# A hybrid S5 and retention decoder layer: first-stage loads one k-tile at a time, fused sine and cosine polynomials, squares moved to ScalarE, earlier side work

## The chip, the cores and the metric

The kernel runs on one core of one Trainium2 chip. The metric is the device time of one execution in microseconds (us); the median of the runs is compared. The engines are TensorE (PE for its matmuls, PEld for its weight loads), VectorE (DVE), ScalarE (ACT), GpSimd (POOL) and SyncE (SP), which here only issues DMAs. Each engine executes its own instructions in the order of the program and waits on semaphores for the others.

## The reference

One decoder layer on 256 prompt positions and on 8 sequences of 8 new positions each, 320 columns in all, at a model width of 2048:

```
h = rms_norm(x, norm_mix)
u, q, k, v, g = split(h @ w_in)
lam_bar = exp(lam * exp(log_step))                 # complex, 64 groups x 64 states
b_bar   = ((lam_bar - 1) / lam) * b
s5      = scan over positions of x' = lam_bar * x + b_bar u;  y = Re(c x) + d * u; gelu; sigmoid GLU
ret     = chunked retention, 8 heads, rotary q and k, group norm, silu(g) gate
x = x + concat(s5, ret) @ w_out
x = x + (silu(gate) * up) @ w_ffn_out              # gate, up = rms_norm(x) @ w_ffn_in
return rms_norm(x), the S5 end states, the retention end states
```

## The kernel before, in words

**Matmuls.** Activations lie transposed: 128 features by 320 columns. Each fp32 weight block `raw` is split into a rounded part `hi` (a copy by ACT) and the rest `lo = raw - hi` (by DVE), the activations likewise into `xhi` and `xlo`; a product is three matmuls: hi with xhi, hi with xlo, lo with xhi. `wload` (L124) and `gemm` (L139) do this for eight k-tiles at a time. The rings `raw`, `hi` and `lo` have three buffers each.

**First stage** (L929 to L957). Four column blocks of `w_in` are accumulated at once over 16 k-tiles of 128 input features: 12 matmuls per k-tile, into `py`, the two halves of `pb`, and `ps_p`. Per step SP loads `x` into `xrs` (the tiles `u32` and `retp`) and then the weights into `raw`; ACT makes `xhi` (L272), `hi` (L943) and the squares for the norm (L277); DVE makes `xlo` (L273), `lo` (L944) and adds the squares up in `u32` (L279 to L288). The steps are the k-tiles 0, 1, then pairs. SP's order in this loop is the order of the code, so a weight load that waits for its `raw` buffer holds the loads behind it. After the loop, PE runs two k-tiles of the next product, `ps_pv`, then six small matmuls `ps_r` that sum the squares (L205), then the rest of `ps_pv`.

**S5 parameters beside it.** `s5_exps` (L374) runs 47 POOL instructions on 128x32 values: 23 for `dt_ = exp(log_step)`, one product, 23 for `rr = exp(lam_re * dt_)`. `s5_params` (L383) makes angles from `dt_` and their sines and cosines with polynomials on DVE; `s5_params2` and `s5_params3` (L423, L435) make the powers `lp`, `gp`, `ff` and the fourth power `r4` of `rr`. `first_states` (L472) multiplies the start states by a power on POOL into `lx0`; it is a generator that runs when a clock of the program, `clk`, reaches `T0 + 12`.

**What sets the order.** PE and POOL run in the order of the code. ACT, DVE, and SP outside the first loop, are ordered when the program is built, by priorities (`tc.high_priority(offset=...)`) and an estimate of when inputs are ready. `tc.issue_after(i)` keeps instructions behind `i` on the engine of `i`. The built order is fixed; on the chip an engine whose next instruction waits holds all that stands behind it.

**Later places of the change.** `do_k` (L876) copies the new columns of k to `ksp` on POOL, which `head_k` (L718) multiplies on PE. `s5_chunk` (L579) runs for eight chunks c; SP shifts a Toeplitz tile `toe` with six small DMAs (L649), loads `yc` from DRAM with eight (L683), and PE multiplies `toe` (L660). The tail (L1356 to L1414) normalises and stores three row tiles; `scale` (L1348) is shared out between DVE and POOL, and `keep_warm(12)` (L1397) fills PE while the last root is computed.

Of the kernel before, what the change touches and what calls it, by code (L numbers as in the profile page):

```python
# [46 lines left out]
def hybrid_kernel(ctx, tc, xT, w_in, w_in4, w_out, w_glu, w_fi, w_fo, w_fot, gfr, vecs, s5p, bc, x0,  # L47
# [335 lines left out]
    def s5_params(dt_):  # L383
# [21 lines left out]
        tt(q, q, ang, MUL)
        tt(es[:, 0::3], q, par, MUL)
        q = T(she)
        ts(q, a2, -1.0 / factorial(14), MUL, 1.0 / factorial(12), ADD)
        for kk in (10, 8, 6, 4, 2, 0):
            tt(q, q, a2, MUL)  # L410
            ts(q, q, (1.0 if (kk // 2) % 2 == 0 else -1.0) / factorial(kk), ADD)
        tt(ec[:, 0::3], q, par, MUL)
        for l in range(2):
# [9 lines left out]
    def s5_params2(used):  # L423
        newscr(1)
        scr[1] = used
        tt(lp[:, 0, 0], rr, ec[:, 0], MUL)
        tt(lp[:, 1, 0], rr, es[:, 0], MUL)
        den = tt(T(sh), prm[:, 0], prm[:, 0], MUL)
        d2 = tt(T(sh), prm[:, 1], prm[:, 1], MUL)
        tt(den, den, d2, ADD)  # L430
        rden = T(sh)
        dve.reciprocal(rden, den)
        rot_t["rden"] = rden

    def s5_params3():  # L435
        rden = rot_t["rden"]
        nr = ts(T(sh), lp[:, 0, 0], -1.0, ADD)
        t1 = tt(T(sh), nr, prm[:, 0], MUL)
# [19 lines left out]

        def ri(t, i):
            return (t[:, 0, i], t[:, 1, i])  # L460

        def rep_(t, n):
            return tuple(t[:, q].unsqueeze(1).to_broadcast([P, n, NPAIR]) for q in range(2))

        cmul(ri(lp, 1), ri(lp, 0), ri(lp, 0), sh)
        cmul(ri(lp, slice(2, 4)), rep_(lp[:, :, 1], 2), ri(lp, slice(0, 2)), [P, 2, NPAIR])
        cmul(ri(gp, slice(0, 3)), rep_(ff, 3), ri(lp, slice(0, 3)), [P, 3, NPAIR])

# [110 lines left out]
    def s5_chunk(c):  # L579
# [64 lines left out]
        with tc.high_priority(offset=EVAC):  # L644
            act.copy(toe[:, :, CH - 1], pk_[:, 0:64].rearrange("p (q h) -> p q h", h=16))
        for u in range(2):
            for t in range(CH - 1):
                d = 16 * (CH - 1 - t)
                sp.dma_start(toe[64 * u + d:64 * u + 64, :, t], toe[64 * u:64 * u + 64 - d, :, CH - 1])  # L649
        with tc.high_priority(offset=2 * EVAC if c == 7 else 0):  # L650
# [28 lines left out]
        yc = s5.tile([P, CH, NC], F32, name="yc", tag="yc", bufs=1)  # L679
        for j in range(4):  # L680
            for g in range(2):
                r = 32 * j + 16 * g
                sp.dma_start(yc[r:r + 16], back[j % 2, :, :, j // 2, g].rearrange("t h c -> h t c"))  # L683
        yield DL["y"]
# [59 lines left out]
    def head_v(h, v_, qg, rt, R):  # L744
# [611 lines left out]
    with tail_order:  # L1356
# [39 lines left out]
        store(1, 0, 5)  # L1396
# [120 lines left out]
```

## Time and profile before

| | |
|---|---|
| runs shown, us | 1429.81, 1428.19, 1428.51: median 1428.51 |
| the profiled execution's own time, us | 1427.82 |
| its span, first to last instruction, us | 1426.0 (1.82 lie around it) |
| granted TensorE clock, mean | 0.999 |
| DVE, ACT, POOL busy | 958.0, 606.4, 124.6 us |
| DMA queue q1 | 264.91 MB, 55.9% of 16 engines |

How to read it: the share of busy time is an average over the stages of the kernel. What a change in one stage can bring is read from the waits of the engine that sets the end in that stage, and from the timeline around them. Times in the timeline are us from the start of the span, then the duration; in brackets is the idle time before the instruction and what ended it. In a table of groups stand busy time and mean ns of one, then the idle time before them. In a table of windows stand, for each engine, busy us and the number of instructions, then the granted clock as a share.

### The profile page before, as it was taken

To read this page: it belongs to the slowest core of one execution; us is meant where nothing else is said; L and a number is where in the kernel's file an instruction comes from. 1 tells how busy PE (TensorE), PEld (TensorE's weight loads), DVE (VectorE), ACT (ScalarE), POOL (GpSimd) and SP (SyncE) were. 2 spreads that over 40 slices of the span, in tenths; PEclk is the share of its full clock that TensorE was granted. 3 is DMA by queue.
4 is the path that set the end of the run, shared out by engine and by line. 5 is a ranking of instruction groups with operands and counts; after the bars stand their busy time and mean duration, and the time that the engine had idled before them with its cause. 6 is when DMAs were issued, how large, how long until landed. Compare 5 with 4: busy or idle time off the path is not lost.

```text
span 1426.0 us, 26198 instructions
## 1 busy us (share of the span) xinstructions
PE 1416.9 (99%) x10376; PEld 1406.4 (99%) x10376; DVE 958.0 (67%) x1852; ACT 606.4 (43%) x965; POOL 124.6 (9%) x194
## 2 busy tenths in 40 slices
PE   9999999999999999999999999999999999999998
PEld 8999999999999999999999999999999999999998
DVE  7978888787657756777777545767744677645453
ACT  7645555555445443333333333333333333333452
POOL 7530021110000000000001000000000000000002
PEclk9999999999999999999999999999999999999999
DMA  8555555556544466675656446666545765455442
GB/s 289 172 170 167 159 174 154 172 163 205 169 154 149 164 207 229 222 254 199 245 201 236 136 147 240 233 213 240 167 144 183 252 230 188 154 165 179 150 142 74
DMA packets 102315, 267.07 MB, mean 187 GB/s; under 512 B 27376, under 2 KB 42160, under 8 KB 102192
## 3 DMA queue, kind: packets, MB, share of 16 engines
q1 hardware_dynamic: 101824, 264.91, 55.9%
q8 instruction: 81, 1.33, 0.4%
q10 hardware_dynamic: 368, 0.49, 0.1%
q14 instruction: 42, 0.34, 0.1%
HBM read 254.44 MB, written 10.52 MB: 186 GB/s over the span
## 4 chain that ended last, share of the span: by engine, by line
PE 76%; DVE 1%; issue 0%; ACT 0%; DMA 0%; SPq 0%; DVEq 0%; ACTq 0%
PE ps_fu L146 7%; PE ps_fg L146 7%; PE ps_fg L145 7%; PE ps_fu L145 7%; PE ps_fg L147 7%; PE ps_fu L147 7%; PE ps_fo L146 7%; PE ps_fo L145 7%; PE ps_fo L147 7%; PE ps_o L145 2%; PE ps_o L147 2%; PE ps_o L146 2%; PE ps_t L1315 1%; PE ps_g L147 1%; PE ps_g L145 1%; PE ps_g L146 1%
## 5 line engine op out<-in xcount | busy, mean ns | idle before, releaser
L133 ACT CAST hi<-raw 128x1024 fp32r<-128x1024 f32 (+1 forms) x410 | 397.8, 971 | 680.9 <-PE ps_fg L146 184.8
L135 DVE TENSOR_TENSOR lo<-raw,hi 128x1024 fp32r<-128x1024 f32 (+1 forms) x410 | 462.2, 1128 | 303.9 <-ACT hi L133 301.8
L147 PE MATMUL ps_fg<-hhi,lo 128*128 128x320 f32 x704 | 217.5, 309 | 0.0
L145 PE MATMUL ps_fg<-hhi,hi 128*128 128x320 f32 x704 | 217.5, 309 | 0.0
L146 PE MATMUL ps_fg<-hlo,hi 128*128 128x320 f32 x704 | 217.5, 309 | 0.0
L146 PE MATMUL ps_fu<-hlo,hi 128*128 128x320 f32 x704 | 217.5, 309 | 0.0
L145 PE MATMUL ps_fu<-hhi,hi 128*128 128x320 f32 x704 | 217.5, 309 | 0.0
L147 PE MATMUL ps_fu<-hhi,lo 128*128 128x320 f32 x704 | 217.5, 309 | 0.0
L145 PE MATMUL ps_fo<-ahl,hi 128*128 128x320 f32 x671 | 207.6, 309 | 0.0
L146 PE MATMUL ps_fo<-ahl,hi 128*128 128x320 f32 x671 | 207.3, 309 | 0.0
L147 PE MATMUL ps_fo<-ahl,lo 128*128 128x320 f32 x671 | 207.3, 309 | 0.0
L145 PE MATMUL ps_p<-xhi,hi 128*128 128x320 f32 x560 | 177.3, 317 | 0.0
L147 PE MATMUL ps_p<-xhi,lo 128*128 128x320 f32 x560 | 173.0, 309 | 0.0
L146 PE MATMUL ps_p<-xlo,hi 128*128 128x320 f32 x560 | 172.8, 309 | 0.0
L147 PEld LDWEIGHTS ps_fg<-hhi,lo 128*128 128x128 f32 x704 | 132.1, 188 | 0.0
L146 PEld LDWEIGHTS ps_fg<-hlo,hi 128*128 128x128 f32 x704 | 132.1, 188 | 0.0
L145 PEld LDWEIGHTS ps_fu<-hhi,hi 128*128 128x128 f32 x704 | 132.1, 188 | 0.0
L146 PEld LDWEIGHTS ps_fu<-hlo,hi 128*128 128x128 f32 x704 | 132.1, 188 | 0.0
L147 PEld LDWEIGHTS ps_fu<-hhi,lo 128*128 128x128 f32 x704 | 132.1, 188 | 0.0
L145 PEld LDWEIGHTS ps_fg<-hhi,hi 128*128 128x128 f32 x704 | 132.1, 188 | 0.0
L146 PEld LDWEIGHTS ps_fo<-ahl,hi 128*128 128x128 f32 x671 | 126.0, 188 | 0.0
L145 PEld LDWEIGHTS ps_fo<-ahl,hi 128*128 128x128 f32 x671 | 125.9, 188 | 0.0
(497 smaller groups left out, 2118.2 us busy)
## 6 DMA issues: line engine op xcount, KB each, us to landing
raw<-w_fi SPq DMA_DIRECT2D x176, 512.0 KB, 4.2
raw<-w_in SPq DMA_DIRECT2D x79, 512.0 KB, 4.1
raw<-w_fo SPq DMA_DIRECT2D x61, 512.0 KB, 3.4
raw<-w_out SPq DMA_DIRECT2D x32, 512.0 KB, 3.7
hi<-vd SPq DMA_DIRECT2D x32, 512.0 KB, 5.5
lo<-vd SPq DMA_DIRECT2D x32, 512.0 KB, 5.2
raw<-w_fo SPq DMA_DIRECT2D x61, 192.0 KB, 2.4
rt<-r SPq DMA_DIRECT2D x8, 512.0 KB, 5.6
```

Of the source, the lines that this page charges most:

```text
L133: cast = act.copy(hi[:, :m], raw[:, :m])
L135: last_lo[0] = dve.tensor_tensor(lo[:, :m], raw[:, :m], f(hi[:, :m]), SUB)
L145: pe.matmul(ps, hi, xhi[:, k], start=k == 0, stop=False)
L146: pe.matmul(ps, hi, xlo[:, k], start=False, stop=False)
L147: pe.matmul(ps, lo, xhi[:, k], start=False, stop=k == nk - 1)
L1315: pe.matmul(ps[0:m, 0:TC], a3[:, x_, k, s:s + m], w_[:, k], start=k == 0 and x_ == 0 and w_ is whi, stop=k == FCT - 1 and w_ is wlo)
```

## The change

Six edits in one:

1. The first stage's steps are k-tiles 0, 1, 2, 3 singly, then pairs (numbers from 0). From k-tile 4 on, SP issues the weight load ahead of the x load.
2. The polynomials of sine and cosine use one DVE instruction a term (add, then multiply) in place of two; the products in `s5_params3` are done with fewer and larger instructions.
3. Four squares go from DVE to ACT: two of `prm`, and `rr` twice to `r4`. They are written in `s5_params2`, so ahead of `s5_params3`.
4. `first_states` is called at head 0's group norm and has no time of its own any more.
5. The `toe` DMAs of the last chunk and the `yc` DMAs of chunk 6 get priority.
6. In the tail `scale` is shared 4, 5 and 4 blocks in place of 5, 5 and 3, and `keep_warm` is 10.

`s5_params` was and is held behind `los[4]`; in the list of `lo` instructions that was k-tiles 6 and 7, and with two more entries it is k-tiles 4 and 5.

```diff
-        q = T(she)
-        ts(q, a2, 1.0 / factorial(13), MUL, -1.0 / factorial(11), ADD)
-        for kk in (9, 7, 5, 3, 1):
-            tt(q, q, a2, MUL)
-            ts(q, q, (1.0 if (kk // 2) % 2 == 0 else -1.0) / factorial(kk), ADD)
...
+        tt(ang, ang, par, MUL)
+        for dst, top, last in ((es, 13, ang), (ec, 14, par)):
+            q = ts(T(she), a2, (-1.0) ** (top // 2) / factorial(top), MUL)
+            for kk in range(top - 2, 1, -2):
+                stt(q, q, (-1.0) ** (kk // 2) / factorial(kk), a2, ADD, MUL)
+            stt(dst[:, 0::3], q, 1.0, last, ADD, MUL)
...
-        den = tt(T(sh), prm[:, 0], prm[:, 0], MUL)
-        d2 = tt(T(sh), prm[:, 1], prm[:, 1], MUL)
+        den, d2 = T(sh), T(sh)
+        act.activation(den, prm[:, 0], AF.Square)
+        act.activation(d2, prm[:, 1], AF.Square)
+        act.activation(r4, rr, AF.Square)
+        act.activation(r4, r4, AF.Square)
...
-        r2 = tt(T(sh), rr, rr, MUL)
-        tt(r4, r2, r2, MUL)
...
         def first_states():
-
-            yield max(0.0, T0 + 12.0 - clk.now)
             newscr(0)
...
-        spawn(first_states())
+        rot_t["first"] = first_states
...
+        with tc.high_priority(offset=3 * EVAC if c == 7 else 0):
+            for u in range(2):
+                for t in range(CH - 1):
+                    d = 16 * (CH - 1 - t)
+                    sp.dma_start(toe[64 * u + d:64 * u + 64, :, t], toe[64 * u:64 * u + 64 - d, :, CH - 1])
...
+        with tc.high_priority(offset=3 * EVAC if c == 6 else 0):
+            for j in range(4):
...
         pool.tensor_tensor(w_, m_, y_, MUL)
+        if h == 0:
+            rot_t["first"]()
...
-    for k1 in (1, *range(2, KT + 1, 2)):
+    for k1 in (1, 2, 3, *range(4, KT + 1, 2)):
...
-            sp.dma_start(xrs[k0 // 4][:, k0 % 4:(k1 - 1) % 4 + 1], xT[:, k0:k1])
+            def load_x():
+                sp.dma_start(xrs[k0 // 4][:, k0 % 4:(k1 - 1) % 4 + 1], xT[:, k0:k1])
+
+            if k0 < 4:
+                load_x()
             (sp if k0 else act).dma_start(raw[:, q], w_in4[:, k0:k1])
+            if k0 >= 4:
+                load_x()
...
-        scale(dve, 1, 0, 5, pb1)
-        scale(pool, 1, 5, 10, rbt[1])
+        scale(dve, 1, 0, 4, pb1)
+        scale(pool, 1, 4, 9, rbt[1])
...
-        keep_warm(12)
+        keep_warm(10)
...
-        scale(dve, 1, 10, NF, pb1)
+        scale(dve, 1, 9, NF, pb1)
```

**ACT in the first stage.** Before, ACT's rows from the `xhi` of k-tiles 8 and 9 on (`retp` holds the x of k-tiles 8 to 15; `hi<-raw` of 1024 values is a pair's weights; `retp<-retp` is a square for the norm):

```order
L272 ACTIVATE xhi<-retp,vec 128x320 [waits DMAHW4_49]
L272 ACTIVATE xhi<-retp,vec 128x320
L943 CAST hi<-raw 128x1024 [waits DMAHW5_49,PE_49]
L277 ACTIVATE retp<-retp 128x640 [waits DVE_49]
L272 ACTIVATE xhi<-retp,vec 128x320 [waits DMAHW6_49]
L272 ACTIVATE xhi<-retp,vec 128x320
```

The same place after the change (L948 is the cast, L424 and L425 the squares that make `r4`, printed as `r_126`):

```order
L272 ACTIVATE xhi<-retp,vec 128x320 [waits DMAHW7_49]
L272 ACTIVATE xhi<-retp,vec 128x320
L424 ACTIVATE r_126<-rr 128x32 [waits Pool_49]
L948 CAST hi<-raw 128x1024 [waits DMAHW0_49,PE_49]
L277 ACTIVATE retp<-retp 128x640 [waits DVE_49]
L272 ACTIVATE xhi<-retp,vec 128x320 [waits DMAHW1_49]
L272 ACTIVATE xhi<-retp,vec 128x320
L425 ACTIVATE r_126<-r_126 128x32 [waits Activation_49]
```

From k-tile 4 on a pair's cast now stands ahead of its `xhi`, where before it stood behind: the first cast of the first piece is that of k-tiles 8 and 9, the first of the second piece that of k-tiles 10 and 11. Ahead of the latter now stands a square that reads `rr`, POOL's last result of `s5_exps`.

**DVE in the first stage.** Before, DVE's rows from the `xlo` of k-tiles 6 and 7 on:

```order
L273 SCALAR_TENSOR_TENSOR xlo<-u_119,vec,xhi 128x320 [waits DMAHW2_49,Activation_49]
L273 SCALAR_TENSOR_TENSOR xlo<-u_119,vec,xhi 128x320 [waits Activation_49]
L944 TENSOR_TENSOR lo<-raw,hi 128x1024 [waits DVE_49,DMAHW3_49,PE_49,Activation_49]
L273 SCALAR_TENSOR_TENSOR xlo<-retp,vec,xhi 128x320 [waits DMAHW4_49,Activation_49]
L273 SCALAR_TENSOR_TENSOR xlo<-retp,vec,xhi 128x320 [waits Activation_49]
```

After the change (`scrt<-prm,scrt` is the first angle, `lam_im * dt_`; before, it stood behind the `lo` of the loop's last pair):

```order
L273 SCALAR_TENSOR_TENSOR xlo<-u_119,vec,xhi 128x320 [waits DMAHW5_49,Activation_49]
L273 SCALAR_TENSOR_TENSOR xlo<-u_119,vec,xhi 128x320 [waits Activation_49]
L180 TENSOR_TENSOR scrt<-prm,scrt 128x32 [waits DMAHW1_49,Pool_49]
L174 TENSOR_SCALAR scrt<-scrt 128x32 [waits DVE_49]
L174 TENSOR_SCALAR scrt<-scrt 128x32
L176 TENSOR_SCALAR scrt<-scrt 128x96 [waits DVE_49]
L949 TENSOR_TENSOR lo<-raw,hi 128x1024 [waits DMAHW6_49,PE_49,Activation_49]
L273 SCALAR_TENSOR_TENSOR xlo<-retp,vec,xhi 128x320 [waits DMAHW7_49,Activation_49]
```

Four small instructions, the first of which waits for POOL's `dt_`, now stand ahead of the `lo` of k-tiles 8 and 9.

**POOL at the change from head 0 to head 1.** Before (`gy` is head 0's group norm, `qsp` and `ksp` are head 1's copies, the rows on `scrt` and `lx_133` are `first_states`):

```order
L794 TENSOR_TENSOR gy<-mv,gy 128x2
L867 COPY qsp<-q__1059 128x64
L452 TENSOR_TENSOR scrt<-x0t,lp 128x256
L453 TENSOR_TENSOR scrt<-x0t,lp 128x256
L454 TENSOR_TENSOR lx_133<-scrt 128x256
L455 TENSOR_TENSOR scrt<-x0t,lp 128x256
L456 TENSOR_TENSOR scrt<-x0t,lp 128x256
L457 TENSOR_TENSOR lx_133<-scrt 128x256
L880 TENSOR_TENSOR kvf<-k__1142,kdt 128x64
L882 COPY ksp<-k__1142 128x64
```

After the change:

```order
L791 TENSOR_TENSOR gy<-mv,gy 128x2
L445 TENSOR_TENSOR scrt<-x0t,lp 128x256
L446 TENSOR_TENSOR scrt<-x0t,lp 128x256
L447 TENSOR_TENSOR lx_133<-scrt 128x256
L448 TENSOR_TENSOR scrt<-x0t,lp 128x256
L449 TENSOR_TENSOR scrt<-x0t,lp 128x256
L450 TENSOR_TENSOR lx_133<-scrt 128x256
L866 COPY qsp<-q__1054 128x64
L879 TENSOR_TENSOR kvf<-k__1131,kdt 128x64
L881 COPY ksp<-k__1131 128x64
```

The six instructions of `first_states` moved ahead of head 1's `qsp`. PE's order is the same as before but for two matmuls of `keep_warm`.

More of the change, by code (lines that the diff above doesn't have):

```diff
@@ L399, in s5_params @@
         a2 = tt(T(she), ang, ang, MUL)
-        q = T(she)
-        ts(q, a2, 1.0 / factorial(13), MUL, -1.0 / factorial(11), ADD)
-        for kk in (9, 7, 5, 3, 1):
-            tt(q, q, a2, MUL)
-            ts(q, q, (1.0 if (kk // 2) % 2 == 0 else -1.0) / factorial(kk), ADD)
[L405 to L412, printed above, removed]
+        tt(ang, ang, par, MUL)
[4 more added lines that the diff above has]
+            stt(dst[:, 0::3], q, 1.0, last, ADD, MUL)
         for l in range(2):
@@ L436, in s5_params3 @@
         rden = rot_t["rden"]
-        nr = ts(T(sh), lp[:, 0, 0], -1.0, ADD)
-        t1 = tt(T(sh), nr, prm[:, 0], MUL)
+        t1 = stt(T(sh), lp[:, 0, 0], -1.0, prm[:, 0], ADD, MUL)
         t2 = tt(T(sh), lp[:, 1, 0], prm[:, 1], MUL)
@@ L442, in s5_params3 @@
         t3 = tt(T(sh), lp[:, 1, 0], prm[:, 0], MUL)
-        t4 = tt(T(sh), nr, prm[:, 1], MUL)
+        t4 = stt(T(sh), lp[:, 0, 0], -1.0, prm[:, 1], ADD, MUL)
         tt(t3, t3, t4, SUB)
         tt(ff[:, 1], t3, rden, MUL)
-        r2 = tt(T(sh), rr, rr, MUL)
-        tt(r4, r2, r2, MUL)
         def cmul(o, a, b, shape, tt=tt):
@@ L457, in cmul, with cpow @@
             tt(o[1], u1, u2, ADD)
[L459 to L467, printed above, removed]
+        def cpow(o, a, b, n):
+            used = scr[1]
+            shn = [P, 2, n, NPAIR]
+            u1, u2 = (T([P, 2 * n, NPAIR]).rearrange("p (r n) j -> p r n j", r=2) for _ in range(2))
+            for u, q in ((u1, 0), (u2, 1)):
+                tt(u, a, b[:, q].unsqueeze(1).unsqueeze(1).to_broadcast(shn), MUL)
+            tt(o[:, 0], u1[:, 0], u2[:, 1], SUB)
+            tt(o[:, 1], u1[:, 1], u2[:, 0], ADD)
+            scr[1] = used
+        cpow(lp[:, :, 1:2], lp[:, :, 0:1], lp[:, :, 0], 1)
+        cpow(lp[:, :, 2:4], lp[:, :, 0:2], lp[:, :, 1], 2)
+        cpow(gp, lp[:, :, 0:3], ff, 3)
         def b8(a):
@@ L645, in s5_chunk @@
             act.copy(toe[:, :, CH - 1], pk_[:, 0:64].rearrange("p (q h) -> p q h", h=16))
[L646 to L649, printed above, removed]
+        with tc.high_priority(offset=3 * EVAC if c == 7 else 0):
[3 more added lines that the diff above has]
+                    sp.dma_start(toe[64 * u + d:64 * u + 64, :, t], toe[64 * u:64 * u + 64 - d, :, CH - 1])
         with tc.high_priority(offset=2 * EVAC if c == 7 else 0):
@@ L679, in s5_chunk @@
         yc = s5.tile([P, CH, NC], F32, name="yc", tag="yc", bufs=1)
[L680 to L683, printed above, removed]
+        with tc.high_priority(offset=3 * EVAC if c == 6 else 0):
+            for j in range(4):
+                for g in range(2):
+                    r = 32 * j + 16 * g
+                    sp.dma_start(yc[r:r + 16], back[j % 2, :, :, j // 2, g].rearrange("t h c -> h t c"))
         yield DL["y"]
@@ L1392, in hybrid_kernel @@
         act.copy(rbt[1], pb1[:, 0:P])
-        scale(dve, 1, 0, 5, pb1)
-        scale(pool, 1, 5, 10, rbt[1])
+        scale(dve, 1, 0, 4, pb1)
+        scale(pool, 1, 4, 9, rbt[1])
         tok_out(1, tp_o[1], sp)
-        store(1, 0, 5)
-        keep_warm(12)
+        store(1, 0, 4)
+        keep_warm(10)
         x_, g_ = xo[0][0:ms_], xg[0][0:ms_]
@@ L1400, in hybrid_kernel @@
         act.activation(sqj[0:ms_], x_, AF.Square, accum_out=rs[0:ms_, 2:3])
-        scale(dve, 1, 10, NF, pb1)
-        store(1, 5, 10)
-        store(1, 10, NF)
+        scale(dve, 1, 9, NF, pb1)
+        store(1, 4, 9)
+        store(1, 9, NF)
         pool.tensor_tensor(g_, x_, grow[0:ms_], MUL)
```

## The prediction

> **What bounds the kernel now.** First the page's busy times and then the list of what PE waited for:
>
> ```profile
> PE 1416.9 (99%) x10376; PEld 1406.4 (99%) x10376; DVE 958.0 (67%) x1852; ACT 606.4 (43%) x965; POOL 124.6 (9%) x194
> ```
>
> ```profile
> PE warm_ps L118 <- POOL ones L64: 1.1, 1, 1.1
> PE pss L104 <- POOL ksp L882: 0.9, 1, 0.9
> PE py L953 <- ACT hi L943: 0.6, 1, 0.6
> PE py L104 <- DMA toe<-toe: 0.5, 1, 0.5
> PE py L953 <- DVE xhi L180: 0.3, 1, 0.3
> ```
>
> PE is busy 99% of the span, and these five waits, 3.4 us, are all that it waits for. PE's work stays the same but for two matmuls of `keep_warm`, so the change can take away 3.4 us at most. What it can add has no such limit: any engine that holds up PE costs its whole delay. So what is to be read is whether a new wait reaches PE. The order shows two candidates, both in the first stage, both on POOL's `s5_exps`: an ACT square of `rr` ahead of the cast of k-tiles 10 and 11, and a DVE product with `dt_` ahead of `lo` of k-tiles 8 and 9. Timeline of PE and then of POOL in that stage:
>
> ```profile
> 24.12 0.31 PE L953 MATMUL py<-xhi,hi 128*128 128x320 f32 x1
> ...
> 35.56 0.72 PE L104 MATMUL ps_r<-ones,u 128*128 128x1 f32 x6
> ```
>
> ```profile
> 9.02 0.54 POOL L348 TENSOR_SCALAR scrt<-prm 128x32 f32<-128x32 f32 x1 [4.15 <-DMA prm<-s5p]
> ...
> 12.56 1.14 POOL L358 TENSOR_TENSOR scrt<-scrt 128x32 f32<-128x32 f32 x1
> ...
> 39.41 0.33 POOL L367 TENSOR_TENSOR rr<-scrt 128x32 f32<-128x32 f32 x1
> ```
>
> The 24.12 is the first matmul of k-tile 10, 12 matmuls (1.76 us) a k-tile. POOL needs from 9.02 to 39.74 for the 47 instructions of `s5_exps`, so `rr` comes 15 us after PE begins k-tile 10. Nobody on PE's path waited for it before; now ACT does.
>
> **When `rr` will be ready.** POOL's pace is not fixed. One DVE row from the stretch of the POOL row at 12.56, and the groups of POOL in a stretch without large DVE work on two SBUF inputs (33.3 to 36.35):
>
> ```profile
> 12.36 1.23 DVE L944 TENSOR_TENSOR lo<-raw,hi 128x1024 fp32r<-128x1024 f32 x1 [0.37 <-ACT hi L943]
> ```
>
> ```profile
> L346 POOL TENSOR_SCALAR scrt<-scrt 128x32 f32<-128x32 f32 x4 | 1.2, 308 | 0.4
> L361 POOL TENSOR_TENSOR scrt<-scrt 128x32 f32<-128x32 f32 x4 | 1.1, 275 | 0.3
> ```
>
> Undisturbed, 8 instructions take 3.0 us, 0.375 each. The one at 12.56 lasted 1.14 and ended just behind a DVE `lo` (12.36 to 13.59): each such `lo` costs POOL about 0.85. With DVE held at its product, the large DVE instructions stay away too, so POOL will run near its free pace. 47 x 0.375 = 17.6; held up before and behind DVE's own wait by three paired `lo` (2.5), the 1280-wide addition (1.1), the short `lo` of k-tiles 2 and 3 (0.6) and some `xlo` (0.6): 4.8. From 9.1, **`rr` at 31.5**; `dt_`, 23 instructions with 2.9 of that, at 20.6. The held-up part is the estimate here; half of it either way is 2.4 us.
>
> The Trainium skill ("SBUF — State Buffer", section "SBUF: two separate sides") says that DVE and GpSimd share one port pair, held exclusively for a whole instruction, by DVE too when it has two SBUF inputs. The pair of rows at 12.36 and 12.56 agrees; by the rule a DVE that waits frees POOL, which is the faster `rr` here, where POOL at its old mean pace would be rival B.
>
> **The new wait on ACT.** ACT's rows of three consecutive kinds:
>
> ```profile
> 17.19 1.05 ACT L943 CAST hi<-raw 128x1024 fp32r<-128x1024 f32 x1 [0.84 <-DMA raw<-w_in]
> 18.15 0.73 ACT L277 ACTIVATE retp<-retp 128x640 f32<-128x640 f32 x1
> 18.79 1.00 ACT L272 ACTIVATE xhi<-retp,vec 128x320 fp32r<-128x320 f32 x2
> ```
>
> Starts lie 0.96 behind a cast and 0.64 behind a square; one `xhi` is 0.5. ACT reaches the square of `rr` when the `xhi` of k-tiles 8 and 9 are done, near 20, and waits there some 11 us. Behind it stand the cast of k-tiles 10 and 11, a square and the `xhi` of k-tile 10, then everything of k-tiles 12 to 15. PE needs the `xhi` for its first matmul: 31.5 + about 0.25 (the small square; DVE's 128x32 product took 0.24) + 0.96 + 0.64 + 0.55 = **33.9 for k-tile 10 in place of 24.12, +9.8**. DVE's own hold, to about 20.6, puts `lo` and `xlo` of k-tile 8 at 21.2 to 22.9, where PE wanted the `xlo` at 21.2: up to 2 us, but PE waits for k-tile 10 anyway, so it adds nothing.
>
> **What follows the wait.** From 24.12 to 35.56 PE had 11.44 us of work to `ps_r`; without more that gives 33.9 + 11.44 = 45.3. Two things can make it later. One is the clock:
>
> ```profile
> 1421.00:1424.40 3.40, 0.00 (x0) 0.00 (x0) 0.61 (x2) 0.27 (x1) 0.56 (x1) 1.00 0.55 153
> 1424.50:1426.00 1.50, 0.00 (x0) 0.00 (x0) 0.00 (x0) 0.00 (x0) 0.00 (x0) 0.50 0.00 0
> ```
>
> ```profile
> 1.12 3.65 PE L118 MATMUL warm_ps<-ones 128*128 128x512 f32 x8 [1.12 <-POOL ones L64]
> ```
>
> ```profile
> 1417.22 2.92 PE L118 MATMUL warm_ps<-ones 128*128 128x512 f32 x12
> 1420.08 0.43 PE L1339 MATMUL ps_b<-ident,ahl 64*128 64x64 f32 x2
> ```
>
> In the first two rows (length, busy times, then PEclk) PE has no matmul from 1420.5 on: the clock is still full for 3.4 us and half from 1424.5. At the start the first eight warm-up matmuls took 3.65 us, 0.46 each, at the end twelve took 2.92, 0.24 each. Eight us of idle would therefore bring half clock, for about as long as at the start: some 3.4 us in which half the work is done, +1.7, so 47.0. The other is DVE, which has work for every k-tile:
>
> ```profile
> L944 DVE TENSOR_TENSOR lo<-raw,hi 128x1024 fp32r<-128x1024 f32 x7 | 8.6, 1229 | 1.4 <-ACT hi L943 1.4
> L273 DVE SCALAR_TENSOR_TENSOR xlo<-u,vec,xhi 128x320 fp32r<-128x320 f32 x8 | 4.1, 546 | 1.0 <-ACT xhi L272 1.0
> ...
> L180 DVE TENSOR_TENSOR u<-u,retp 128x640 f32<-128x640 f32 x2 | 1.6, 821 | 0.0
> ...
> L180 DVE TENSOR_TENSOR u<-u 128x320 f32<-128x320 f32 x1 | 0.5, 476 | 0.0
> ```
>
> ACT ends the `xhi` of k-tile 14 at about 39.2 (33.9, then an `xhi`, the second small square, two casts, two squares and three `xhi`). Then DVE has two `xlo`, `lo`, an addition of 640, `lo` of the next product, two more such additions, its second `lo`, small work, and the last addition of 320: by distances of starts (0.08 below these means) 7.2 us, so `ps_r`'s input stands at 46.4 whatever PE does. That is a floor of 46.4 - 35.56 = 10.9; with the half clock 11.5. I take **+11.4**.
>
> The Trainium skill ("TensorE: Matmul & The Clock Gate", section "What's actually happening") gives half clock after at least one idle window of about 3.4 us, and full clock after about 3.4 us of work; the trace's 3.4 to 3.9 and the start's 3.65 agree. By it the delay is 47.0 - 35.56 = 11.5; without a clock loss it is the floor, 10.9.
>
> **What the other edits take away.** The step by single k-tiles brings `hi` of k-tile 2 earlier, at most the 0.6 us wait on `hi` at 9.86; but a later wait that ends at a fixed time swallows whatever PE gains ahead of it, so 0. `pss`, 0.9 us: POOL at head 1:
>
> ```profile
> 74.94 3.85 POOL L867 COPY qsp<-q__1059 128x64 f32<-128x64 f32 x1 [8.26 <-DVE q__1059 L180]
> 78.75 0.63 POOL L452 TENSOR_TENSOR scrt<-x0t,lp 128x256 f32<-128x256 f32 x1
> ...
> 84.42 0.72 POOL L457 TENSOR_TENSOR lx<-scrt 128x256 f32<-128x256 f32 x1
> ```
>
> `first_states` (78.75 to 85.1, 6.4 us) moves into the 8.26 us in which POOL waited for `q`; `ksp` comes some 6 us earlier, the whole 0.9 goes. `toe`, 0.5 us, in ACT's row and the chain of waits:
>
> ```profile
> 331.45 0.21 ACT L645 COPY toe<-pk__4711 128x64 f32<-128x64 f32 x1 [0.81 <-PE pk__4711 L104]
> ```
>
> ```profile
> 339.85 0.59 SPq L649
> 340.49 2.12 DMA toe<-toe
> ```
>
> Six issues of 0.6 directly behind 331.7 end at 335.3, plus 2.1: 337.4; before, the last transfer ended at 342.6. The weight loads behind these six issues go out 3.6 us later. PE's list has no wait for a weight load, so they have some slack; if none, the edit gains nothing or costs up to 3.6 - 0.5 = 3.1. I take -0.5, since three buffers of weights lie between such a load and its use. In the tail a block less in the 0.81 us `scale` of 5 blocks:
>
> ```profile
> 1416.85 0.81 DVE L1350 TENSOR_TENSOR ahl<-x,ps_b 128x640 f32<-128x640 f32 x1
> ```
>
> 0.16 us, and two warm-up matmuls of 0.24 that can stand ahead of the end; -0.15, between 0 and -0.6. The 21 fewer small DVE instructions (about 0.2 each) lie between 33 and 58 us where PE waited for nothing from DVE: 0. Weights ahead of inputs change only what lands first in k-tiles 4 to 15, and PE had no wait for either: 0.
>
> **Sum**, against the profiled execution's own 1427.82 (span 1426.0 and 1.82 around it): 1427.82 + 11.4 - 0.9 - 0.5 - 0.15 = 1437.7. The median of the runs is 0.7 above that execution, so 1438.4; rounded to **1438.0**.
>
> **Rivals.**
> A, not slower, the other side: ACT isn't held. ACT has until 24.12 - 2.4 = 21.7 before PE notices; `rr` would need 47 instructions in 12.7 us, 0.27 each, below the undisturbed 0.375. It would take a much faster POOL, or a square that stands elsewhere on the chip than in the order. Then the gains alone are left: 1427.82 - 0.6 - 0.9 - 0.5 - 0.15 = 1425.7, 1426.4 as a median. 0.05.
> C: only DVE's hold counts, +1.7 in place of 11.4: 1428. Same condition for ACT; 0.04.
> B: POOL keeps its old mean pace (30.7 us for 47) although DVE is idle: `rr` at 39.8, +8.3: 1446.3. The row at 12.56 against its neighbours speaks against it; 0.06.
> D: the norm that follows `ps_r` is a chain on DVE, now crowded with the polynomials that are late too; two to six small DVE rows of 0.24 between its links add 0.5 to 1.5: 1439.5. 0.12.
> E: half clock for a second such stretch, since the waits for DVE leave PE idle in between: +1.7, 1440. 0.10.
> The forecast keeps 0.63.
>
> **How the numbers follow.** Low end: `rr` earlier by the 2.4 of the estimate and a clock loss that DVE's floor hides, rounded up for the part of it that PE would not see: 1434.5. High end: the same 2.4 late with part of D or E: 1442. Outside lie A, C and B, 0.15, and a little of the forecast's own. A measurement of this kernel can tell about 0.2%, 2.9 us, from no change. Faster by more than that: only A with more gain than worked out, 0.02. Within: the rest of A, and C, 0.07. Slower: 0.91.
>
> **What would show it.** In the changed kernel's list of waits: PE `py` <- ACT `xhi` or `hi` of 7 to 8 us near 26 to 34, ACT idle about 11 us before L424 released by POOL, and DVE idle about 2 us before `scrt<-prm,scrt`. POOL's `rr` near 31.5: that tests the pace; near 40 means B, before 22 means A. PEclk at half for some 3 us behind 34 tests the 1.7. `ps_r` near 47.0; no wait on `ksp` and on `toe`. The prediction is wrong if the square's wait is shorter than 10 us, or if PE loses more behind `ps_r` than it gains later.

## The result, and the profile after

| | before | changed |
|---|---|---|
| median of 5 runs, us | 1428.19 (1427.92 to 1429.81) | 1440.12 (1439.77 to 1442.86) |
| ratio, 95% interval | | 1.0085 (1.0071 to 1.0099) |
| span of the profiled execution, us | 1426.0 | 1437.7 |
| mean granted TensorE clock | 0.999 | 0.996 |

The change costs 12 us, 0.85%. The page of the changed kernel, its busy times:

```profile
PE 1419.6 (99%) x10374; PEld 1408.3 (98%) x10374; DVE 955.9 (66%) x1831; ACT 606.8 (42%) x970; POOL 113.7 (8%) x194
```

PE's share is 99% as before. Twelve us are 0.8% of the span; a share doesn't show them. What PE waited for, in the changed kernel (us in total, times, longest):

```profile
PE py L958 <- ACT xhi L272: 7.3, 1, 7.3
PE py L958 <- DVE xlo L273: 1.9, 2, 1.8
PE pst L109 <- DVE k__735 L180: 1.3, 1, 1.3
PE warm_ps L118 <- POOL ones L64: 1.1, 1, 1.1
PE ps_o L164 <- DVE r4b L180: 0.4, 1, 0.4
PE pst L109 <- ACT kd L723: 0.3, 1, 0.3
PE py L958 <- ACT hi L948: 0.2, 1, 0.2
```

The waits on `ksp` and `toe` are gone. New ones are `xhi` (7.3), `xlo` (1.9), `k` (1.3), `r4b` (0.4) and `kd` (0.3). The timeline of PE in the changed kernel at the places of the first chain (start, duration; in brackets the wait):

```profile
33.48 0.63 PE L958 MATMUL py<-xhi,hi 128*128 128x320 f32 x1 [7.30 <-ACT xhi L272]
...
47.55 0.72 PE L104 MATMUL ps_r<-ones,u 128*128 128x1 f32 x6
...
66.16 0.41 PE L109 MATMUL pst<-ident,k__735 128*128 128x128 f32 x2 [1.28 <-DVE k__735 L180]
...
67.49 0.33 PE L109 MATMUL pst<-ident,v__741 128*128 128x128 f32 x1 [0.26 <-ACT kd L723]
```

K-tile 10 starts at 33.48 in place of 24.12. PE's matmuls come in the same order in both kernels (but for the two of `keep_warm`), so the start of the same matmul can be compared all the way through the program. This is the distance of the changed kernel behind the one before:

| matmul | before, us | changed, us | distance | step |
|---|---|---|---|---|
| first of k-tile 10 | 24.12 | 33.48 | 9.36 | +9.36 |
| `ps_r` | 35.56 | 47.55 | 11.99 | +2.63 |
| `pst` of `v` | 53.83 | 67.49 | 13.66 | +1.67 |
| `pss` of head 1 (`ksp`) | 85.65 | 98.22 | 12.57 | -1.09 |
| `py` ahead of `toe` | 342.06 | 354.42 | 12.36 | -0.21 |
| `py` on `toe` | 342.74 | 354.52 | 11.78 | -0.58 |
| `ps_o` on `r4b` | 347.49 | 359.69 | 12.20 | +0.42 |
| last `ps_b` | 1420.08 | 1431.94 | 11.86 | -0.34 |

Nearly all of it arises within the first 50 us. POOL and then ACT in the changed kernel:

```profile
9.45 0.69 POOL L348 TENSOR_SCALAR scrt<-prm 128x32 f32<-128x32 f32 x1 [4.57 <-DMA prm<-s5p]
...
20.31 0.25 POOL L367 TENSOR_TENSOR scrt<-scrt 128x32 f32<-128x32 f32 x1
...
30.89 0.25 POOL L367 TENSOR_TENSOR rr<-scrt 128x32 f32<-128x32 f32 x1
```

```profile
18.22 1.00 ACT L272 ACTIVATE xhi<-retp,vec 128x320 fp32r<-128x320 f32 x2
31.17 0.23 ACT L424 ACTIVATE r<-rr 128x32 f32<-128x32 f32 x1 [11.95 <-POOL rr L367]
31.31 1.03 ACT L948 CAST hi<-raw 128x1024 fp32r<-128x1024 f32 x1
32.24 0.73 ACT L277 ACTIVATE retp<-retp 128x640 f32<-128x640 f32 x1
32.88 1.00 ACT L272 ACTIVATE xhi<-retp,vec 128x320 fp32r<-128x320 f32 x2
```

A square of 0.23 us makes ACT stand for 11.95 us, with the cast of k-tiles 10 and 11 behind it. DVE stands twice, for `dt_` and then for ACT:

```profile
20.60 0.19 DVE L180 TENSOR_TENSOR scrt<-prm,scrt 128x32 f32<-128x32 f32 x1 [3.23 <-POOL scrt L367]
...
32.37 1.22 DVE L949 TENSOR_TENSOR lo<-raw,hi 128x1024 fp32r<-128x1024 f32 x1 [7.56 <-ACT hi L948]
```

And the clock, in windows of the changed kernel (length, busy time and number of instructions of PE, PEld, DVE, ACT and POOL, then PEclk, DMA share and GB/s):

```profile
28.50:29.00 0.50, 0.00 (x0) 0.00 (x0) 0.00 (x0) 0.00 (x0) 0.39 (x2) 0.86 0.00 0
29.00:30.00 1.00, 0.00 (x0) 0.00 (x0) 0.00 (x0) 0.00 (x0) 0.74 (x4) 0.50 0.00 0
...
38.50:39.00 0.50, 0.50 (x4) 0.50 (x4) 0.48 (x2) 0.45 (x1) 0.00 (x0) 0.50 0.93 246
39.00:39.50 0.50, 0.50 (x5) 0.50 (x5) 0.50 (x3) 0.29 (x1) 0.00 (x0) 0.90 0.75 250
```

From 28.86 (a mean of 0.86 over the half us from 28.5) to 39.1 the clock is at half, 5.6 us of it with PE at work: its matmuls stand 0.267 us apart there, 0.147 at full clock.

### The profile page after: what moved, and what is told of

Same layout as the page of the kernel before. It is cut to its first block, busy times and chain, and to the rows that moved or that the text cites. A ratio compares the mean times of both kernels' runs of the same rounds, so it can differ in the third digit from the quotient of the medians.

```text
span 1437.7 us, 26179 instructions
## 1 busy us (share of the span) xinstructions
PE 1419.6 (99%) x10374; PEld 1408.3 (98%) x10374; DVE 955.9 (66%) x1831; ACT 606.8 (42%) x970; POOL 113.7 (8%) x194
## 4 chain that ended last, share of the span: by engine, by line
PE 94%; DVE 2%; POOL 1%; DMA 1%; issue 1%; ACT 1%; SPq 0%; DVEq 0%; ACTq 0%
PE ps_fu L145 7%; PE ps_fg L145 7%; PE ps_fg L147 7%; PE ps_fu L147 7%; PE ps_fg L146 7%; PE ps_fu L146 7%; PE ps_fo L145 7%; PE ps_fo L146 7%; PE ps_fo L147 7%; PE ps_p L145 5%; PE ps_p L147 5%; PE ps_p L146 5%; PE ps_o L146 2%; PE ps_o L145 2%; PE ps_o L147 2%; PE ps_t L1320 1%
```

## The experiments

The theory: the square of `rr` holds ACT and with it PE, the half clock adds to that, and the later edits give back one to two us. The rivals: another edit makes the loss (DVE's hold at `dt_`, the order of the loads), and, for the wait on `k` (PE's matmuls `pst`, which transpose `k`, wait for DVE's last product of `k`), the polynomials between the links of DVE's norm chain. Two profiles can differ by about 1 us at the very start, where PE waits for the first loads (in the profiles of before_square_only, first_only and toe_only the second k-tile begins 0.8 to 1.4 us later than in that of the kernel before); so the steps of the distance behind the kernel before are read, more than the spans. The last column has that distance, in us, at three places.

| kernel | time | ratio to before | span, us | distance at `ps_r`, `pst` of `k`, end |
|---|---|---|---|---|
| changed | 1440.12 | 1.0085 (1.0071 to 1.0099) | 1437.7 | 11.99, 13.43, 11.8 |
| sq_on_dve | 1432.61 | 1.0031 (1.0019 to 1.0043) | 1430.7 | 1.71, 5.01, 4.8 |
| hold_late | 1440.30 | 1.0082 (1.0068 to 1.0095) | 1438.6 | 11.36, 12.32, 12.8 |
| both_undone | 1428.09 | 0.9996 (0.9987 to 1.0005) | 1426.6 | -0.39, 0.02, 0.6 |
| before_square_only | 1439.81 | 1.0079 (1.0064 to 1.0094) | 1438.1 | 12.06, 12.06, 12.2 |
| sq_cz_late | 1429.66 | 1.0011 (1.0001 to 1.0020) | 1427.6 | 2.36, 3.36, 1.7 |
| kept_warm | 1441.82 | one run | 1440.0 | 12.68, 15.19, 14.2 |
| kept_warm_2 | 1441.59 | one run | 1439.5 | 9.74, 13.63, 13.7 |
| cz_late | 1438.50 | one run | 1436.4 | 10.96, 12.24, 10.5 |

### Which hold makes the loss

sq_on_dve undoes the square on ACT:

```diff
-        act.activation(r4, rr, AF.Square)
-        act.activation(r4, r4, AF.Square)
...
+        r2 = tt(T(sh), rr, rr, MUL)
+        tt(r4, r2, r2, MUL)
```

> The changed kernel with the two squares of rr back on VectorE at the end of s5_params3; all else as changed. Theory (the square of rr holds ACT, and everything of k-tiles 10 to 15 behind it): PE's 7.3 us wait on xhi is gone and so is the half clock; the DVE hold before the lo of k-tiles 8 and 9 stays, PE waits about 1.8 us for xlo of k-tile 8 near 21; ps_r near 37.4. The later gains (ksp 1.1, toe, tail, together about 1.8) stay: span about 1426, within 0.2% of the kernel before. Rival (the loss comes from the other edits of the first stage, such as the loads' order or the late product on DVE): span stays above 1430.

hold_late undoes the hold on DVE, with ACT's square left; both_undone does both:

```diff
-    with tc.issue_after(los[4].ins):
+    with tc.issue_after(los[6].ins):
```

> The changed kernel with s5_params held behind the lo of k-tiles 8 and 9 in place of 4 and 5, so that the product with dt_ stands behind the loop's last lo, as before; the square of rr stays on ACT. Theory: the ACT hold alone makes the loss, and DVE's hold costs PE nothing. As DVE works on to about 22 in place of idling from 17.4 to 20.6, it takes the port from POOL longer: rr about 32.5 in place of 31.1, ps_r about 1.3 us later than in the changed kernel, span 1438 to 1439.5. Rival (POOL's pace doesn't follow DVE): rr stays near 31 and the span at 1437.7 or below. Rival (DVE's hold is what costs): span below 1432.

> Both of the above: squares of rr on VectorE and s5_params held behind the lo of k-tiles 8 and 9. Theory: no hold is left, DVE keeps busy, so POOL ends rr near 39.5 as before; PE loses nothing up to ps_r (35.2 to 35.6), and what the other edits bring is left: ksp 0.9 to 1.1, toe 0.5 less 0.4 for a new wait on r4b, tail 0.3: span 1424.0 to 1424.6, ratio to the kernel before about 0.999, not told apart from 1 by much. Rival (some other edit costs too): span 1426 or more.

before_square_only is the kernel before with the two squares on ACT, nothing else:

```diff
+        act.activation(r4, rr, AF.Square)
+        act.activation(r4, r4, AF.Square)
...
-        r2 = tt(T(sh), rr, rr, MUL)
-        tt(r4, r2, r2, MUL)
```

> The kernel before with one edit, the two squares of rr on ACT in s5_params2; the built order puts the first behind the xhi of k-tiles 10 and 11, ahead of the cast of k-tiles 12 and 13. Theory: ACT waits for rr there from about 20.6 on; DVE runs out of work near 24 and POOL then runs free, so rr near 33; PE waits for hi or xhi of k-tile 12 from 27.6 to about 34.8, some 7 us, then half clock for 3 to 5 us costs 1.5 to 2.5, and a wait near pst of 1 to 1.6 follows: span 1436 to 1438. Rival (the square costs only its own 0.2 us): span 1426.

The square on ACT alone reproduces the loss: 1.0079 against 1.0085 for the whole change. What PE waited for in before_square_only, first row:

```profile
PE py L953 <- ACT hi L943: 9.5, 3, 7.9
```

The expectation had put it at k-tile 12; it is at k-tile 10 (33.54 in place of 24.12), since before the change a pair's cast stands behind its `xhi`. The half clock adds the same there as in the changed kernel (9.42 at k-tile 10, 12.06 at `ps_r`: 2.64), but no wait on `k` follows, and nothing is given back later. In hold_late the DVE hold is gone and nothing is won over the whole program: the ratio is the same. It is 0.6 us ahead of the changed kernel at `ps_r` and 1.1 at `pst`, and loses that again by waits on `lo` (below); half clock ran from 27.39 to 37.63 there, 1.5 us earlier than in the changed kernel, which by itself makes up about that 0.6. Its `rr` did not come at 32.5 as expected but at the same time as in the changed kernel:

```profile
30.96 0.25 POOL L367 TENSOR_TENSOR rr<-scrt 128x32 f32<-128x32 f32 x1
```

In both kernels the same large DVE instructions run ahead of ACT's hold, only in another order, and POOL runs free for the rest. In these kernels POOL's `rr` comes the earlier the longer DVE stands: 39.74 before and 39.43 in both_undone, where DVE works on; 37.63 in sq_on_dve, where it stands only for `dt_`; 31.1 to 32.3 where it stands behind ACT (the changed kernel, hold_late, before_square_only). ACT, and PE for a part, stand then too, but the changed kernel's rows of `s5_exps` tell them apart: the 31 POOL instructions with nothing on DVE beside them took 0.21 to 0.30 us each, the 9 with ACT at work 0.27 in the mean and the 22 with ACT standing 0.26; the four that mostly met a `lo` of 1024 values took 0.98 in the mean. That POOL's pace follows DVE's work is shown by this; which part of an instruction of DVE's does it is not.

sq_on_dve removed the 7.3 us wait, as the theory had it, but its span is 1430.7 and not 1426: a third wait is there that neither theory had so large. The first two rows of its PE waits:

```profile
PE pst L109 <- DVE k__733 L180: 3.0, 1, 3.0
PE py L958 <- DVE xlo L273: 1.7, 2, 1.5
```

So DVE's hold at `dt_`, for which the prediction had charged nothing, costs 1.7 us at `ps_r` when ACT's hold isn't there to hide it, and then sets off 3.3 us more at `pst`. Against both_undone, which differs by this hold alone, it is 2.1 and 2.9. A part of the loss is the clock again (columns as above):

```profile
59.00:59.50 0.50, 0.44 (x2) 0.44 (x3) 0.50 (x2) 0.01 (x1) 0.50 (x2) 0.55 0.19 53
59.50:62.00 2.50, 2.50 (x12) 2.50 (x11) 2.47 (x15) 1.55 (x4) 1.90 (x8) 0.50 0.61 172
62.00:62.50 0.50, 0.50 (x4) 0.50 (x3) 0.29 (x3) 0.48 (x2) 0.00 (x0) 0.54 0.96 298
```

The 3.0 us wait near 54.7 was enough for half clock, 1.3 us after PE had begun to work again; that costs another 1.4 (5.34 to 6.76 in the distance).

With both undone the kernel can't be told from the one before: 0.9996 (0.9987 to 1.0005). The expected gain of 1.4 to 2 us did not come, and the rival's sign, a span of 1426 or more, did: the span is 1426.6, and the distance, -0.39 at `ps_r`, grows to 1.13 by head 1, since new waits on `kd` (0.5) and `lo` (1.2) outweigh what the `ksp` edit gives back. both_undone keeps the new order of the loads, so that rival is out: this order costs nothing that these runs can tell. No version of this study that was run more than once is faster than the kernel before.

### What the half clock costs

kept_warm fills PE's wait with 24 matmuls nobody reads (its second edit, which holds the `cz` copies, isn't shown):

```diff
+        if k0 == 10:
+            keep_warm(24, warm_t)
         for k in range(k0, k1):
```

> The changed kernel with 24 warm-up matmuls of 512 columns between k-tiles 9 and 10, in PE's wait (24 x 0.24 = 5.6 us from about 26.0 to 31.7); the cz copies on ACT are held behind the third cast of 1024, so that ACT's order there is nearly that of the changed kernel. Theory (idle PE, then half clock, costs 2.5 us of the loss): PEclk stays at 1.00, k-tile 10 starts at about 33.4 as in the changed kernel, its matmuls follow 0.147 apart, and ps_r comes not 2.5 but 1.5 to 2.3 us earlier than 47.5, since DVE's chain of lo, xlo and additions then sets it (about 45.3 to 46); span 1435.2 to 1436.3. Rival (the slow matmuls behind the wait are late operands and not the clock): spacing stays 0.267 and the span 1437.7.

The clock stayed full and the distance stayed within 9.26 to 9.42 up to `ps_pv`'s first product with `lo`. There PE met a new wait of 2.5 us, and half clock came with it (46.88 to 53.71): the built order had moved the polynomials on DVE ahead of the `lo` that it needs. So the span, 1440.0, not the 1435.2 to 1436.3 expected, says nothing of the clock in front. kept_warm_2 holds the polynomials behind those `lo`:

```diff
+    wpv = wload(w_in[10], KT)
     with tc.issue_after(los[4].ins):
         s5_params(exps[0])
...
+        with tc.issue_after(last_lo[0].ins):
             for part in PI_PARTS:
```

> As kept_warm (24 warm-up matmuls in PE's wait), with the polynomials on DVE held behind the two lo of the next product, since in kept_warm the built order had put them ahead and PE waited 2.5 us for lo. Judged by ps_r, not by the span, since DVE's order behind it still differs. Theory (half clock costs 2.5 us up to ps_r, of which DVE's chain would keep a part even at full clock): k-tile 10 at about 33.4, matmuls 0.147 apart, PE waits 0.3 to 1.2 for lo or for u, ps_r at 45.0 to 46.0 in place of 47.5. Rival (the chain of operands sets ps_r, the clock only fills its gaps): ps_r at 47.0 or later.

PE in kept_warm_2, and the clock:

```profile
33.15 0.42 PE L966 MATMUL py<-xhi,hi 128*128 128x320 f32 x1 [1.84 <-ACT xhi L275]
...
45.30 0.72 PE L104 MATMUL ps_r<-ones,u 128*128 128x1 f32 x6
```

```profile
26.00:33.00 7.00, 5.31 (x24) 4.05 (x22) 0.96 (x1) 2.16 (x4) 4.00 (x16) 1.00 0.00 1
33.00:45.00 12.00, 11.55 (x76) 11.25 (x77) 11.39 (x17) 8.86 (x18) 0.00 (x0) 1.00 0.61 186
```

`ps_r` comes at 45.30 and not 47.55: from k-tile 10 to `ps_r` PE needs 12.15 us, against 14.07 in the changed kernel and 11.44 before. So about 1.9 us of the 2.6 go with the half clock, though DVE's order differs a little too; the 0.7 left includes a wait of 0.3 for `lo`. DVE's additions, which the prediction took for a floor of 46.4, ended at 43.4 in this order. But nothing of the 1.9 reached the end: PE waits 2.6 us for `k`, `pst` starts at 66.36 against 66.16 in the changed kernel, and half clock follows (66.86 to 70.27). Here the next wait swallowed it. DVE's order behind `ps_r` isn't the same in the two, so for the changed kernel itself that isn't shown.

### The wait on k

In the changed kernel ACT stood for late loads of `raw_bc` until 48.53 and 51.55 us (1.20 and 1.97 us; before, once for 1.42), with a cast and so DVE's `lo` and `csr` behind them. `csr` are the turning factors, scaled by the norm, that make `q` and `k`. cz_late puts these `cz` copies of ACT behind its copy `rbc`:

```diff
-        for q in range(2):
+        with tc.issue_after(rot_t['rbc'].ins) if c < 2 else contextlib.nullcontext():
+          for q in range(2):
             for g in range(2):
                 act.mul(cl0[64 * g:64 * g + 64, q, :, 16 * g:16 * g + 16],
...
-            act.copy(rbc, rps)
+            rot_t['rbc'] = act.copy(rbc, rps)
```

> The changed kernel with the eight cz copies of the first two chunks on ACT held behind the copy rbc in place of ahead of it. Theory (the second wait of the changed kernel, 1.3 us on k near 64.9, comes from ACT standing at cz for late raw_bc loads, with the cast behind it and so DVE's lo and then csr): ACT no longer idles 2 us near 49.6, csr starts near 54.8 in place of 56.5, the wait on k is gone: span 1436.0 to 1436.5. Rival (the polynomials between the links of DVE's norm chain are the cause, as the prediction's case D had it): nothing moves, 1437.7.

> sq_on_dve (squares of rr on VectorE) with the cz copies held behind rbc as well. Theory: the 3.0 us wait on k near 54.7 falls below 0.6, and with it the half clock from 59 to 62.3 that cost 1.4: span 1426.0 to 1426.8, the DVE hold's 1.7 us against later gains of the same size. Rival (polynomials, or DVE's hold itself, make the wait on k): span 1430 to 1430.7.

In cz_late the wait on `k` went from 1.3 to 1.1 only; the span fell by 1.3 all the same, into the range expected, but by luck. A row of its windows and one of PE show why that is no clean test:

```profile
36.50:37.00 0.50, 0.50 (x5) 0.50 (x4) 0.50 (x2) 0.50 (x2) 0.00 (x0) 0.71 0.04 16
```

```profile
46.52 0.72 PE L104 MATMUL ps_r<-ones,u 128*128 128x1 f32 x6
```

Full clock came back at 36.8 and not 39.1, by its own phase, so PE reached `ps_r` 1.0 earlier. Counted from `ps_r`, `csr` starts 8.10 us later in cz_late, 8.94 in the changed kernel and 7.94 before: of the 1.0 us by which `csr` was late, the `cz` copies account for 0.84. Yet `pst` follows `ps_r` by 18.45, nearly the 18.61 of the changed kernel (17.17 before). So the rest is made behind `csr`. The traces show where (us; `e` are tables that POOL makes from the last polynomial result `ecs`):

| kernel | `csr` starts after `ps_r` | first `e` on POOL after `csr` starts | last `k` ends after `csr` starts |
|---|---|---|---|
| before | 7.94 | 5.24 | 8.20 |
| changed | 8.94 | 0.15 | 9.52 |
| cz_late | 8.10 | 0.15 | 10.20 |
| sq_on_dve | 10.12 | 0.14 | 10.20 |
| sq_cz_late | 8.48 | 0.15 | 9.53 |
| before_square_only | 8.24 | 5.26 | 8.20 |
| hold_late | 10.07 | 4.91 | 7.91 |
| both_undone | 9.50 | 4.92 | 7.93 |

In the changed kernel `csr` comes 1.00 later, `k` takes 1.32 more behind it, and 0.88 of the 1.03 us that `k` had in hand before `pst` is used up: 1.44 together, the step from 11.99 to 13.43. The stretch behind `csr` is long in the four kernels where DVE ends the polynomials ahead of `csr`, and short where `s5_params` is held late (hold_late, both_undone) or stands as before. In the long ones `qg` (another product of `q`) and a reciprocal stand ahead of `k`, and POOL makes its tables beside `q` and `k`. DVE's rows are longer there, first before, then changed:

```profile
48.59 1.22 DVE L135 TENSOR_TENSOR lo<-raw,hi 128x1024 fp32r<-128x1024 f32 x1
...
51.22 0.48 DVE L180 TENSOR_TENSOR k__737<-k__737,sw 128x320 f32<-128x320 f32 x1
```

```profile
62.76 1.46 DVE L135 TENSOR_TENSOR lo<-raw,hi 128x1024 fp32r<-128x1024 f32 x1
...
65.19 0.82 DVE L180 TENSOR_TENSOR k__735<-k__735,sw 128x320 f32<-128x320 f32 x1
```

So this part goes with the early end of the polynomials; no run moves POOL's tables or `qg` alone, so the cause within the stretch is read from rows and not shown by a run. In sq_cz_late the test of the `cz` copies is plainer:

```profile
PE pst L109 <- DVE k__733 L180: 0.7, 1, 0.7
```

The wait falls from 3.0 to 0.7, a little short of the expected 0.6, no half clock follows, and 1.0031 becomes 1.0011. Of the 2.3, 1.6 lie ahead of `csr` and 0.7 behind it. The span, 1427.6, lies between the two ranges that had been set; `ps_r` is 0.65 later than in sq_on_dve. The `cz` copies are most of this wait there, and a part of it in the changed kernel; what the polynomials contribute between the links was not tried by itself.

### Where the gains went

first_only and toe_only are the kernel before with one edit each, `first_states` called at head 0's group norm, and the priority for `toe` and `yc`:

```diff
-            yield max(0.0, T0 + 12.0 - clk.now)
...
-        spawn(first_states())
+        rot_t["first"] = first_states
...
+        if h == 0:
+            rot_t["first"]()
```

> The kernel before with one edit, first_states called at head 0's group norm. Theory: the wait on ksp (0.9 to 1.0) goes, but first_states on POOL now runs beside the large products of chunk 1 on DVE (bl, m, cl, near 66 to 72) and each holds the other up, so the lo behind them come 1.5 to 2.5 us late and PE waits 1.0 to 1.2 for lo near 72 to 75, as in both_undone: span 1425.9 to 1426.4, no gain. Rival (those waits on lo came from another edit): span 1425.0.

The run took 1429.42 us, with a span of 1427.6 and 1.13 of it lost at the start. The `ksp` wait went (0.89 less distance), but two waits on `lo` near 72 and 77 us came (0.62 and 0.73 more). POOL and DVE in first_only, and then DVE at the same place of the kernel before:

```profile
71.36 1.61 POOL L456 TENSOR_TENSOR scrt<-x0t,lp 128x256 f32<-128x256 f32 x1
```

```profile
68.25 1.51 DVE L180 TENSOR_TENSOR bl<-m,m 128x256 f32<-128x256 f32 x2
69.80 1.11 DVE L180 TENSOR_TENSOR m<-raw_bc,lpc 128x512 f32<-128x512 f32 x1
70.83 1.65 DVE L135 TENSOR_TENSOR lo<-raw,hi 128x1024 fp32r<-128x1024 f32 x1
```

```profile
67.27 0.76 DVE L180 TENSOR_TENSOR bl<-m,m 128x256 f32<-128x256 f32 x2
68.06 0.69 DVE L180 TENSOR_TENSOR m<-raw_bc,lpc 128x512 f32<-128x512 f32 x1
68.67 1.22 DVE L135 TENSOR_TENSOR lo<-raw,hi 128x1024 fp32r<-128x1024 f32 x1
```

Beside `first_states` DVE's products take up to twice as long (two `bl` 1.51 in place of 0.76). In the changed kernel the two meet as well:

```profile
77.10 1.66 DVE L180 TENSOR_TENSOR bl<-m,m 128x256 f32<-128x256 f32 x2
78.80 2.15 DVE L180 TENSOR_TENSOR m<-raw_bc,lpc 128x512 f32<-128x512 f32 x2
80.87 1.66 DVE L135 TENSOR_TENSOR lo<-raw,hi 128x1024 fp32r<-128x1024 f32 x1
```

But there PE is further behind DVE: it uses that `lo` at 84.45, 1.9 us after its end, so it doesn't wait, and the gain of 1.09 stays. In both_undone and hold_late they meet without such slack, and the gain is lost (both have 1.2 us of waits on `lo`).

```diff
+        with tc.high_priority(offset=3 * EVAC if c == 7 else 0):
             for u in range(2):
...
+        with tc.high_priority(offset=3 * EVAC if c == 6 else 0):
             for j in range(4):
```

> The kernel before with one edit, the priority for the toe DMAs of chunk 7 and the yc DMAs of chunk 6. Theory: PE's wait on toe at 342.7 (0.5 to 0.7) goes, and a wait for r4b on DVE near 347.5 of 0.2 to 0.6 comes in its place, since DVE's work behind that place didn't become earlier: gain 0.1 to 0.4 behind 348. Rival (the r4b wait comes from another edit): the whole 0.5 to 0.7 stays.

The `toe` wait went and a wait on `r4b` came, as expected:

```profile
PE ps_o L164 <- DVE r4b L180: 0.3, 1, 0.3
```

The distance falls by 0.58 at `toe` and grows by 0.36 at `r4b`: 0.22 net. The run took 1427.98 us; a gain of 0.2 can't be told from none by it.

### A test that missed its object

lock_two and lock_one were to add 14 additions of 128x256 on DVE while it stands for ACT, with two operands in SBUF or with one, to see whether a shared port is what slows POOL.

```diff
+        if k0 == 8:
+            with tc.high_priority(offset=100000), tc.issue_after(los[-1].ins):
+                for _ in range(14):
+                    tt(dm, dm, dm, ADD)
```

> The changed kernel with 14 extra DVE additions of 128x256 (dm = dm + dm, both operands in SBUF) put where DVE idles for ACT, from about 23.5 on; they compute nothing that is used. The built order puts the small DVE work of the polynomials between them. Read by POOL's rr, not by the span. Theory (a DVE instruction with two SBUF operands holds POOL up for its length): POOL instructions that meet one take 0.5 to 0.8 in place of 0.28, rr at 33.5 to 36 in place of 31.1, and k-tile 10 later by as much. Rival (POOL's pace hangs on something else, such as its own code or DMA): rr at 31 to 31.5.

> The same with dm = warm_ps + dm, one operand in PSUM and one in SBUF; the order of DVE's instructions is the same. Theory (only two SBUF operands hold POOL up): the 14 additions cost POOL nothing, only the polynomials between them do: rr at 31.5 to 33.3, at least 1.2 ahead of lock_two. Rival (any DVE work slows POOL): rr within 0.5 of lock_two.

The runs took 1443.80 and 1444.07 us, `rr` came at 30.13 and 29.67. In lock_two DVE ran three of the additions and then stood:

```profile
24.10 0.42 DVE L181 TENSOR_TENSOR dm<-dm 128x256 f32<-128x256 f32 x1
31.36 1.23 DVE L952 TENSOR_TENSOR lo<-raw,hi 128x1024 fp32r<-128x1024 f32 x1 [6.83 <-ACT hi L951]
```

lock_one has `warm_t[:, 0:256]` in place of the first of the two inputs `dm`. The built order had put eleven of the fourteen behind instructions that wait for ACT. The two runs say nothing on the port, and it isn't settled here.

## Why the prediction came out as it did

The direction, the place and the mechanism were as forecast, and 1440.12 lies in the range, 2.1 above the 1438.0. Of its own two signs of being wrong, a square's wait below 10 us is far from the 11.95, but the other was close: behind `ps_r` PE lost 2.09 (1.67 and 0.42) and gained 2.22. Step by step:

- **`rr` at 31.5**: 31.14, and `dt_` at 20.56 for 20.6. The estimate that POOL runs near its free pace while DVE stands was right. That it comes so close is partly luck: from 25.0 to 30.9 the instructions start 0.35 apart and not 0.375, 1.4 us less over 47, against a start 0.35 later and about 0.6 more of being held up than estimated. B, POOL at its old mean pace, would have had 39.8.
- **K-tile 10 at 33.9, +9.8**: 33.48, +9.36; the 0.4 is `rr`.
- **DVE's hold adds nothing**: true beside ACT's hold over the whole program (hold_late is no faster than the changed kernel), though DVE stood 3.23 and not about 2. By itself it costs 1.7 at `ps_r`, as rival C priced it, and sets off 3.3 more at `pst` (sq_on_dve), which C did not have.
- **The half clock, +1.7**: mis-sized. Half clock lasted 10.2 us, 5.6 of them with PE at work, and the distance grew by 2.63 between k-tile 10 and `ps_r`; with the clock kept full it grew by 0.71. The prediction let a half clock of 3.4 us begin when PE began; in the records it has a phase of its own and lasted three such lengths here, two in cz_late. (The 47.0 - 35.56 that the prediction gives as 11.5 is 11.44.) E, the half clock for a second stretch, came near this, but named later waits of PE as the cause.
- **The floor by DVE, 46.4**: it wasn't a floor. DVE's additions ended at 46.17 in the changed kernel but at 43.42 in kept_warm_2, where they stand ahead of the `lo`.
- **D, 0.5 to 1.5 at the next use of the norm**: this happened, with 1.67, and was left out of the forecast's sum as one of the rivals. Its cause as named, polynomials between the links, was not tried alone. What the traces show is late `raw_bc` loads at the head of ACT (0.84 of the 1.00 by which `csr` came late) and 1.32 behind `csr`, which goes with the early end of the polynomials.
- **Gains of 0.9, 0.5 and 0.15**: 1.09, 0.58 and 0.34; but the second is followed by a new wait of 0.42 on `r4b`, so that it nets 0.16 in the changed kernel. The prediction did not ask what is late next there, nor what `first_states` meets on DVE in its new place; the 1.09 stayed only because PE had 1.9 us of slack there.
- **A** (ACT not held): refuted by ACT's 11.95 us, and in the other direction both_undone shows what A would have had: no gain either, 0.9996.

Summed over the distance, half clock and floor were 1.0 too small and the waits on `k` (1.67) and `r4b` (0.42) missing, against 0.4 too much for `rr` and 0.67 more gain than forecast, the 0.21 between 98 and 354 us among it.

## What to carry to other kernels

A small instruction that waits for a slow side chain must not stand ahead of the main chain on an in-order engine: the 0.23 us square cost 12 us, since what stood behind it was the cast that PE needed. Where a scheduler places such instructions, an explicit edge that keeps them behind the urgent work is part of the edit, and the built order is to be read on every engine that got a new instruction. A hold costs more than its length: PE's clock fell, and late loads and side work that had moved made a second wait, on `k`, behind `ps_r`. And work that is moved into an engine's idle time is free only if it doesn't slow another engine on the path at that moment, as `first_states` on POOL slowed DVE in first_only.

## What the runs showed of the hardware

Half clock comes in whole lengths of about 3.4 us on a phase of its own: 28.86 to 39.1 (10.2) in the changed kernel, 29.96 to 36.79 (6.8) in cz_late with the same wait in front, 59.05 to 62.46 (3.4) in sq_on_dve. PE came back at 33.48 in the changed kernel and at 33.50 in cz_late. Counted in lengths of 3.41 us (a third of 39.1 - 28.86) from the start of half clock, that is 1.2 us into the one from 32.27 and full clock came at the end of the next one; in cz_late it is 0.1 us into the one from 33.37 and full clock came at its end. So nearly the same hold cost 1.0 us more at `ps_r` in one than in the other; that one kernel differs so from one execution to the next was not measured. The Trainium skill ("TensorE: Matmul & The Clock Gate", section "What's actually happening") describes a free-running window of about 3.4 us, and the lengths agree with it; it gives at least one idle window as the condition. In sq_on_dve a wait of 3.0 us, less than a window, was enough, and half clock began when PE had been at work again for 1.3 us. Waits of 2.5 us in kept_warm and 2.6 us in kept_warm_2 were enough too; behind the wait of 1.84 us ahead of k-tile 10 in kept_warm_2 the clock stayed full.
